# First linear of a decoder layer: preparing the input one pair of chunks ahead, meta tokens in one transfer, five idle products

## The chip, the cores and the metric

The kernel runs on one core of a Trainium2 chip. A core has a matrix engine (TensorE, PE in the profile; its weight loads are a row of their own, PEld), a vector engine (VectorE, DVE), a scalar engine (ScalarE, ACT), GpSimd (POOL) and SyncE (SP), which here only issues transfers. Each engine runs its own instructions in their order and waits on semaphores for the others. Data lie in SBUF (128 partitions); products go to PSUM, which has eight banks of 128 x 512 float32; 16 DMA engines move data between HBM and SBUF.

The metric is the device time of one execution in microseconds: the median of the runs of the kernel.

## The reference

One layer of a decoder on 256 tokens of width 2048, in float32, with 16 learned meta tokens put ahead of the sequence, so T = 272 rows. Only its beginning matters here: the meta tokens and the input are joined, normalised with a gain, and multiplied with the weights of a SwiGLU block.

```python
s = jnp.concatenate([meta, x], axis=1)               # 16 + 256 rows of 2048
h = rms_norm(s, norm_ffn1[layer])
s = s + 0.5 * swiglu_ffn(h, ffn1_w_gu[layer], ffn1_w_down[layer])
...
def swiglu_ffn(h, w_gu, w_down):
    gate, up = jnp.split(h @ w_gu, 2, axis=-1)
    return (jax.nn.silu(gate) * up) @ w_down
```

After that follow an attention and a convolution mixer, a gated merge, a second SwiGLU block and a last norm. They are the same in both kernels.

## The kernel before

**Layout.** Activations are kept transposed: the 2048 features are 16 chunks of 128, a chunk lies on the 128 partitions and its 272 tokens lie along the free axis. Four tiles `s0` to `s3` hold the residual stream, four chunks each. The input arrives with tokens on the partitions, so each chunk has to be transposed by the PE first.

**Products.** Each float32 operand is split in a rounded part and a rest (`wh` and `wl` for weights, `h` part 0 and part 1 for activations), and a product of the two is made as three matmuls (L280 to L282): `wh` by high, `wh` by low, `wl` by high. The weights come in pairs of chunks (`KB = 2`): for each pair ("block") ACT makes `wh` by a rounding copy (L270) and DVE makes `wl` by a subtraction (L271), each over 128 x 1024. A block of `linear` is then 2 chunks x 4 output tiles x 3 = 24 matmuls of 272 columns. The first linear, `pg`, goes over all 16 chunks: 8 blocks, 192 matmuls into four banks. The next one, `pu`, has the same shape.

**Preparing the input.** The first linear alone gets `before=before1`. Ahead of the weight split of each block, `before1` prepares the two chunks of that very block with `prep` (L579): a transpose of 16 x 128 of the meta tokens (`xm`, L582), two transposes of 128 x 128 of the input (`xin`, L584), all into one bank `pt`; one copy of 272 columns by DVE into `s` (L585); then `gain_split` (L172): ACT scales by the gain and rounds (L176), DVE makes the rest (L177). The split of the block's weights is held behind the second chunk's copy and scaling (`issue_after`). For every block but the first, `before1` also adds the squares of the two chunks prepared in the block before (`norm1.add`: square on ACT, L193, addition on DVE, L195). The order in which these instructions then stand on each engine is made by a scheduler, which takes instructions ahead where banks and data allow; so the transposes of chunks 2 to 8 stand together between the first and the second block.

**Transfers at the start.** ACT's queue issues the gain of the first norm (`grow`) and then the meta tokens, two transfers of 16 partitions x 1024 (L83). SP's queue issues the first half of the first `xin` tiles (chunks 0 to 3), the weights of block 0, chunks 4 to 7, the weights of blocks 1 to 4, then chunks 8 to 15 (`load_x`, L75), then the weights on, as their five buffers `st` come free.

**Idle products.** At the very start six matmuls of the identity with itself (`WARM = 6`, L64 to L66; each is two rows in the trace) keep the PE at work until the first data have come. Their result is not used.

The sum of squares ends in a matmul with ones (`ssq_ps`, L200) behind the last product of `pg`. A transpose of small vectors, `vp` (L130, `make_vec`), is one of the side steps which the scheduler puts among the products.

Of the kernel before, what the change touches and what calls it, by code (L numbers as in the profile page):

```python
# [9 lines left out]
F32 = mybir.dt.float32  # L10
# [5 lines left out]
P = 128  # L16
D = 2048
SEQ = 256
NMETA = 16
T = SEQ + NMETA  # L20
F = 5632
DC = D // P
GC = 4
GW = GC * P
W2 = D // 2
# [9 lines left out]
N_ACT = 24  # L35
EVICT_AT = 1
WARM = 6
HOLD = 3
LATER_AT = (4, 6)
KINDS = "DDSDDSDS"  # L40
# [4 lines left out]
def decoder_layer(ctx: ExitStack, tc: tile.TileContext, t, out):  # L45
    nc = tc.nc
# [3 lines left out]
    apool = ctx.enter_context(tc.tile_pool(name="a", bufs=N_ACT))  # L50
# [3 lines left out]
    def bank(name):  # L54
        return psum.tile([P, 512], F32, tag="acc", name=name)
# [4 lines left out]
    ident = const.tile([P, P], F32, name="ident")  # L60
# [1 line left out]


    warm = bank("warm")  # L64
    for _ in range(WARM):
        nc.tensor.matmul(warm[:, :P], ident, ident, start=True, stop=True)  # L66


    grow = const.tile([DC, P], F32, name="grow")
    nc.scalar.dma_start(out=grow, in_=t["norm_ffn1"][0].rearrange("(c p) -> c p", p=P))  # L70
    x = t["x"][0]
    xm = [apool.tile([NMETA, W2], F32, tag="act", name=f"xm{q}") for q in range(2)]
    xin = [[apool.tile([P, W2], F32, tag="act", name=f"xin{q}{i}") for i in range(2)] for q in range(2)]

    def load_x(k):  # L75

        q, cs = k // 2, slice(k % 2 * GW, (k % 2 + 1) * GW)
        for i in range(2):
            nc.sync.dma_start(out=xin[q][i][:, cs], in_=x[i * P : (i + 1) * P, k * GW : (k + 1) * GW])

    load_x(0)
    for q in range(2):
        nc.scalar.dma_start(out=xm[q], in_=t["meta_tokens"][:, q * W2 : (q + 1) * W2])  # L83

    NV = 2 * DC + 3 * NH + 1
    vrows = const.tile([NV, P], F32, name="vrows")
# [2 lines left out]
    def load_gain(g0, src):  # L89
# [5 lines left out]
        out=vrows[G_CONV:G_SUB, :], in_=t["conv_w"][0].rearrange("k (c p) -> (k c) p", p=P)  # L95
# [3 lines left out]
    for i, n in enumerate(("lambda_q1", "lambda_k1", "lambda_q2", "lambda_k2")):  # L99
# [7 lines left out]
        out=mask[:, T - P :],  # L107
        in_=mask[:, T - P :],
# [24 lines left out]
    def make_lam():  # L133
        lprod = tmp.tile([P, 2, HD], F32, tag="lprod", bufs=1, name="lprod")
        nc.vector.tensor_mul(lprod, lamv[:, 0:4:2, :], lamv[:, 1:4:2, :])
        ldot = const.tile([P, 2], F32, name="ldot")
        nc.vector.tensor_reduce(out=ldot, in_=lprod, axis=AX.X, op=ALU.add)
        lexp = const.tile([P, 2], F32, name="lexp")
        nc.scalar.activation(lexp, ldot, AF.Exp)
        nc.vector.tensor_sub(lam, lexp[:, 0:1], lexp[:, 1:2])  # L140
        nc.vector.tensor_scalar_add(lam, lam, LAM_INIT)
        nc.vector.tensor_scalar_mul(subg, col(G_SUB), 1.0 - LAM_INIT)


    sF = [apool.tile([P, GC, T], F32, tag="act", name=f"s{g}") for g in range(DC // GC)]

    def s(c, t0, t1=T):
        return sF[c // GC][:, c % GC, t0:t1]
# [23 lines left out]
    def gain_split(h, c, gain):  # L172

        w = h.width
        hi, lo = h.part(c, 0, 0, w), h.part(c, 1, 0, w)
        a = nc.scalar.mul(hi, s(c, T - w), gain)  # L176
        b = nc.vector.scalar_tensor_tensor(  # L177
            out=lo, in0=s(c, T - w), scalar=gain, in1=hi.bitcast(F32), op0=ALU.mult, op1=ALU.subtract
        )
        return a.ins, b.ins  # L180
# [59 lines left out]
    def drain(n=0):  # L240
        while len(ahead) > n:
            ahead.pop(0)()

    def linear(act, chunks, w, k0, c0, t0, t1, name, evict, before=None, side_at=(5, 9, 13)):

        n = t1 - t0
        kb = KB
        nl = kb if before is not None else LB * kb  # L250
        acc = [bank(f"{name}_{j}") for j in range(GC)]
        for b in range(0, len(chunks), kb):
            blk = chunks[b : b + kb]
            r0 = (k0 + blk[0]) * P
            wh = wpool.tile([P, kb, GW], F32R, tag="wh", name="wh")
            wl = wpool.tile([P, kb, GW], F32R, tag="wl", name="wl")
            m = len(blk)
            if b % nl == 0:
                st = wpool.tile([P, LB * kb, GW], F32, tag="st", bufs=ST_BUFS, name="st")
                ml = min(nl, len(chunks) - b)  # L260
                nc.sync.dma_start(
                    out=st[:, :ml, :],
                    in_=w[r0 : r0 + ml * P, c0 : c0 + GW].rearrange("(c p) f -> p c f", p=P),
                )
            sw = st[:, b % nl : b % nl + m, :]
            with ExitStack() as order:
                if before is not None:
                    for ins in before(blk):
                        order.enter_context(tc.issue_after(ins))
                nc.scalar.copy(out=wh[:, :m, :], in_=sw)  # L270
                nc.vector.tensor_sub(wl[:, :m, :], sw, wh[:, :m, :].bitcast(F32))  # L271
            drain()
            for i, c in enumerate(blk):
                first, last = b + i == 0, b + i == len(chunks) - 1
                for j in range(GC):
                    a, f = acc[j][:, :n], slice(j * P, (j + 1) * P)
                    if 2 * n <= 512:
                        nc.tensor.matmul(acc[j][:, : 2 * n], wh[:, i, f], act.both(c, t0, t1), start=first, stop=False)  # L278
                    else:
                        nc.tensor.matmul(a, wh[:, i, f], act.part(c, 0, t0, t1), start=first, stop=False)  # L280
                        nc.tensor.matmul(a, wh[:, i, f], act.part(c, 1, t0, t1), start=False, stop=False)  # L281
                    nc.tensor.matmul(a, wl[:, i, f], act.part(c, 0, t0, t1), start=False, stop=last)  # L282
                if b + i == EVICT_AT:
                    flush()
                if b + i in LATER_AT and later:
                    later.pop(0)()
                if b + i in side_at and side:
                    side.pop(0)()
        flush()
        pending.append(lambda: evict(acc))  # L290
# [10 lines left out]
    def flush():  # L301
        while pending:
            pending.pop(0)()
# [272 lines left out]
    h1 = Act("h1", DC, T)  # L576
    norm1 = Norm(0, "1")

    def prep(c):  # L579
        pt = bank("pt")  # L580
        q, cs = c // NH, slice(c % NH * P, (c % NH + 1) * P)
        nc.tensor.transpose(pt[:, :NMETA], xm[q][:, cs], ident[:NMETA, :NMETA])  # L582
        for i in range(2):
            nc.tensor.transpose(pt[:, NMETA + i * P : NMETA + (i + 1) * P], xin[q][i][:, cs], ident)  # L584
        v = nc.vector.tensor_copy(s(c, 0), pt[:, :T])  # L585
        a, b = gain_split(h1, c, gain1[:, c : c + 1])
        return a, v.ins

    def before1(blk):


        c = blk[0]
        if c // 2 + 1 < 4:
            load_x(c // 2 + 1)
        r = []
        for k in blk:
            a, v = prep(k)
            r = [a, v]
        if c:
            for k in blk:  # L600
                norm1.add(k - 2)
        if c == DC - 2:
            for k in blk:
                norm1.add(k)
            pending.append(norm1.end)
            side.append(make_vec)

            def lam_step():
                with tc.issue_after(norm1.last.ins):
                    make_lam()  # L610

            side.append(lam_step)
        return r
# [12 lines left out]
    for half in halves:  # L626
        m = gate_up(h1, half, t["ffn1_w_gu"][0], norm1, 0, before1 if half is halves[0] else None)
        for c in range(0, DC, GC):

            def down(pd, c=c, final=half is halves[-1]):  # L630
                for j in range(GC):
                    nc.vector.scalar_tensor_tensor(
                        out=s(c + j, 0), in0=pd[j][:, :T], scalar=0.5, in1=s(c + j, 0), op0=ALU.mult, op1=ALU.add
                    )
                    if final:
                        after1(c + j)

            linear(m, list(range(len(half) * GC)), t["ffn1_w_down"][0], half[0] * GC, c * P, 0, T, "pd", down)
# [283 lines left out]
    for half in thirds:  # L922
# [10 lines left out]
        if final:  # L933
            for q in range(2):
                nc.gpsimd.dma_start(
                    out=gfin[q],
                    in_=t["norm_final"][q * W2 : (q + 1) * W2].rearrange("(o d) -> o d", o=1).to_broadcast([P, W2]),
                )
        for u in range(2):
# [12 lines left out]

            hold = HOLD if final and u else 0
            linear_tok(
# [30 lines left out]
```

## Time and profile before

| | |
|---|---|
| median of 3 runs | 2220.5 us (2220.43 to 2220.69) |
| time of the profiled execution | 2221.51 us |
| its span, first to last instruction | 2219.7 us |
| PE busy | 2201.4 us, 99% of the span |
| DVE busy | 1404.4 us, 63% |
| ACT busy | 1018.4 us, 46% |
| DMA | 401.96 MB, mean 181 GB/s |

The time of the profiled execution is 1.8 us more than its span: what lies before the first and after the last instruction. A row of a timeline gives start, duration, engine, source line, operation, output from inputs with their shapes, and the number of instructions merged in it. A row of the chain of waits gives start, the length of the piece that lies on the chain, engine, tile and line. A row of the windows gives the stretch, its length, and for each engine its busy time and, in brackets, its instructions. Instructions of one engine overlap: the duration of one is its latency, and the distance between the starts of two is what the engine takes for one in a stream.

### The profile page before, as it was taken

Reading aid. Unit: us, or ns where it says so; the run is one execution under the profiler, and the core shown is the slowest. Engines: PE = TensorE matmul, PEld = TensorE weight load, DVE = VectorE, ACT = ScalarE, POOL = GpSimd, SP = SyncE. Lnnn points to the kernel's source line nnn. Section 1 sums busy time; section 2 is a strip of 40 time slices with the busy share of each in tenths; the row PEclk is TensorE's granted clock in tenths of the full one; section 3 lists DMA queues with packets and bytes.
Section 4 is the critical chain, followed back from the end, with each engine's and each line's share of the span. In section 5 each row is a group of like instructions: output and inputs, shape, how many; then the busy total and the mean of one; then the engine's idle time right before and its main releaser. Section 6 shows DMA issues by size and latency. Waiting matters only on the chain.

```text
span 2219.7 us, 33148 instructions
## 1 busy us (share of the span) xinstructions
PE 2201.4 (99%) x13578; PEld 1984.4 (89%) x13578; DVE 1404.4 (63%) x1845; ACT 1018.4 (46%) x1265; POOL 6.4 (0%) x17
## 2 busy tenths in 40 slices
PE   9999999999999999999999999999999999999998
PEld 8999999999999999898988888888878887888886
DVE  7555554455555565567765544679886688856985
ACT  6343433334343443444444444456554455534554
POOL 0000000000000000000000000000000000000000
PEclk9999999999999999999999999999999999999999
DMA  7555555555555555444555555554566455664562
GB/s 252 171 177 180 176 171 172 179 179 174 171 173 178 180 173 172 161 143 152 166 180 191 190 186 189 189 180 151 196 211 211 169 193 190 224 211 171 190 228 95
DMA packets 192024, 401.96 MB, mean 181 GB/s; under 512 B 8676, under 2 KB 8736, under 8 KB 191872
## 3 DMA queue, kind: packets, MB, share of 16 engines
q1 hardware_dynamic: 191232, 398.49, 53.0%
q8 instruction: 106, 1.74, 0.3%
q0 software_dynamic: 544, 1.21, 0.2%
q14 instruction: 46, 0.38, 0.0%
q10 hardware_dynamic: 96, 0.14, 0.0%
HBM read 397.71 MB, written 2.10 MB: 180 GB/s over the span
## 4 chain that ended last, share of the span: by engine, by line
PE 93%; DVE 4%; issue 1%; DMA 1%; ACT 1%; POOL 0%; SPq 0%; DVEq 0%; POOLq 0%; ACTq 0%
PE pg L468 4%; PE pg L467 4%; PE pg L466 4%; PE pg L282 4%; PE pg L280 4%; PE pd L282 4%; PE pu L282 4%; PE pu L280 4%; PE pg L281 4%; PE pd L280 4%; PE pd L281 4%; PE pu L281 4%; PE pd L320 4%; PE pd L318 4%; PE pd L319 4%; PE o L278 3%
## 5 line engine op out<-in xcount | busy, mean ns | idle before, releaser
L271 DVE TENSOR_TENSOR wl<-st,wh 128x1024 fp32r<-128x1024 f32 x392 | 478.6, 1224 | 442.3 <-ACT wh L270 442.0
L270 ACT CAST wh<-st 128x1024 fp32r<-128x1024 f32 x392 | 411.3, 1050 | 613.9 <-PE pd L281 146.9
L370 DVE TENSOR_TENSOR wl<-st,wh 128x1024 fp32r<-128x1024 f32 (+1 forms) x360 | 420.5, 1177 | 253.4 <-ACT wh L369 252.4
L369 ACT CAST wh<-st 128x1024 fp32r<-128x1024 f32 (+1 forms) x360 | 365.4, 1018 | 431.2 <-PE pd L319 132.3
L280 PE MATMUL pg<-h,wh 128*128 128x272 f32 x704 | 203.7, 290 | 2.0 <-ACT wh L270 2.0
L280 PE MATMUL pu<-h,wh 128*128 128x272 f32 x704 | 203.2, 289 | 0.0
L282 PE MATMUL pu<-h,wl 128*128 128x272 f32 x704 | 203.0, 288 | 0.0
L282 PE MATMUL pd<-m,wl 128*128 128x272 f32 x704 | 203.0, 288 | 0.0
L280 PE MATMUL pd<-m,wh 128*128 128x272 f32 x704 | 202.9, 288 | 0.0
L281 PE MATMUL pg<-h,wh 128*128 128x272 f32 x704 | 202.6, 289 | 0.0
L281 PE MATMUL pd<-m,wh 128*128 128x272 f32 x704 | 202.4, 288 | 0.0
L281 PE MATMUL pu<-h,wh 128*128 128x272 f32 x704 | 202.4, 288 | 0.0
L282 PE MATMUL pg<-h,wl 128*128 128x272 f32 x704 | 201.3, 290 | 0.0
L467 PE MATMUL pg<-wh,hn 128*128 128x512 f32 x390 | 151.9, 389 | 0.0
L466 PE MATMUL pg<-wh,hn 128*128 128x512 f32 x390 | 151.2, 389 | 0.0
L468 PE MATMUL pg<-wl,hn 128*128 128x512 f32 x390 | 144.1, 392 | 1.0 <-DVE wl L370 0.8
L318 PE MATMUL pd<-wh,m 128*128 128x512 f32 x352 | 137.5, 391 | 0.0
L319 PE MATMUL pd<-wh,m 128*128 128x512 f32 x352 | 137.0, 389 | 0.0
L320 PE MATMUL pd<-wl,m 128*128 128x512 f32 x352 | 135.8, 390 | 0.0
L280 PEld LDWEIGHTS pg<-h,wh 128*128 128x128 f32 x704 | 133.3, 189 | 2.4 <-ACT wh L270 2.4
L281 PEld LDWEIGHTS pg<-h,wh 128*128 128x128 f32 x704 | 133.8, 190 | 0.0
L281 PEld LDWEIGHTS pu<-h,wh 128*128 128x128 f32 x704 | 132.7, 189 | 0.0
(277 smaller groups left out, 4615.6 us busy)
## 6 DMA issues: line engine op xcount, KB each, us to landing
st<-in_ffn_w_gu_dram SPq DMA_DIRECT2D x184, 512.0 KB, 4.4
st<-in_ffn_w_down_dram SPq DMA_DIRECT2D x88, 1024.0 KB, 5.1
st<-in_ffn_w_gu_dram SPq DMA_DIRECT2D x84, 1024.0 KB, 4.9
st<-in_w_in_dram SPq DMA_DIRECT2D x48, 1024.0 KB, 5.1
st<-in_w_gate_dram SPq DMA_DIRECT2D x64, 512.0 KB, 4.1
st<-in_w_branch_dram SPq DMA_DIRECT2D x32, 512.0 KB, 4.4
st<-in_w_out_dram SPq DMA_DIRECT2D x16, 1024.0 KB, 5.0
xin<-in_x_dram SPq DMA_DIRECT2D x8, 256.0 KB, 7.9
```

The costliest lines, as they stand in the source:

```text
L270: nc.scalar.copy(out=wh[:, :m, :], in_=sw)
L271: nc.vector.tensor_sub(wl[:, :m, :], sw, wh[:, :m, :].bitcast(F32))
L280: nc.tensor.matmul(a, wh[:, i, f], act.part(c, 0, t0, t1), start=first, stop=False)
L281: nc.tensor.matmul(a, wh[:, i, f], act.part(c, 1, t0, t1), start=False, stop=False)
L282: nc.tensor.matmul(a, wl[:, i, f], act.part(c, 0, t0, t1), start=False, stop=last)
L318: nc.tensor.matmul(ps, hi, wh[:, q, :], start=first, stop=False)
L319: nc.tensor.matmul(ps, lo, wh[:, q, :], start=False, stop=False)
L369: nc.scalar.copy(out=wh, in_=src)
L370: nc.vector.tensor_sub(wl, src, wh.bitcast(F32))
L466: nc.tensor.matmul(ps[k], hi, wh, start=first, stop=False)
L467: nc.tensor.matmul(ps[k], lo, wh, start=False, stop=False)
L468: nc.tensor.matmul(ps[k], hi, wl, start=False, stop=left[k] == 0)
```

## The change

Four edits, all in the first linear and ahead of it:

- The meta tokens come in one transfer over all 128 partitions (row `t*8 + g` of `xm` holds 256 features of token `t`). Two transposes of 128 x 128 into a bank `pm` turn all of them at once; `prep_meta` copies them to the first 16 columns of the four chunks of one `s` tile by two small strided copies, once for every four chunks. `prep` then transposes and copies only the 256 tokens of the input.
- `linear` asks for the chunks of the next block right behind the weight split of the present one (`ready`), so transposes, scaling and splits of the input run one pair ahead, and no block but the first has its own preparation in front of it. For block 0 two pairs are prepared before its products.
- Five more idle products stand behind the transposes of chunks 2 and 3 (`WARM_PREP = 5`).
- The copies of chunks 2 and 3 out of PSUM are held behind the split of chunk 1 (`issue_after(split_of[1])`); the later halves of the input are asked for in the calls of chunks 2, 4 and 6 rather than 0, 2 and 4.

```diff
+WARM_PREP = 5
...
-    for _ in range(WARM):
-        nc.tensor.matmul(warm[:, :P], ident, ident, start=True, stop=True)
+    def keep_warm(n):
+        for _ in range(n):
+            nc.tensor.matmul(warm[:, :P], ident, ident, start=True, stop=True)
+
+    keep_warm(WARM)
...
-    xm = [apool.tile([NMETA, W2], F32, tag="act", name=f"xm{q}") for q in range(2)]
+    xm = apool.tile([P, 2 * P], F32, tag="act", name="xm")
...
-    for q in range(2):
-        nc.scalar.dma_start(out=xm[q], in_=t["meta_tokens"][:, q * W2 : (q + 1) * W2])
+    nc.scalar.dma_start(out=xm, in_=t["meta_tokens"].rearrange("t (g f) -> (t g) f", f=2 * P))
...
+        ready = {}
         for b in range(0, len(chunks), kb):
...
-                    for ins in before(blk):
+                    for ins in ready.pop(b) if b else before(blk):
                         order.enter_context(tc.issue_after(ins))
                 nc.scalar.copy(out=wh[:, :m, :], in_=sw)
                 nc.vector.tensor_sub(wl[:, :m, :], sw, wh[:, :m, :].bitcast(F32))
+            if before is not None and b + kb < len(chunks):
+                ready[b + kb] = before(chunks[b + kb : b + 2 * kb])
...
+    pm, split_of = [], []
+
+    def prep_meta(g):
+
+        if not pm:
+            pm.append(bank("pm"))
+            for j in range(2):
+                nc.tensor.transpose(pm[0][:, j * P : (j + 1) * P], xm[:, j * P : (j + 1) * P], ident)
+        for j in range(2):
+            cols = pm[0][:, j * P : (j + 1) * P].rearrange("p (t g) -> p g t", t=NMETA)
+            nc.vector.tensor_copy(sF[g][:, j:GC:2, :NMETA], cols[:, 2 * g : 2 * g + 2, :])
+
     def prep(c):
         pt = bank("pt")
         q, cs = c // NH, slice(c % NH * P, (c % NH + 1) * P)
-        nc.tensor.transpose(pt[:, :NMETA], xm[q][:, cs], ident[:NMETA, :NMETA])
         for i in range(2):
-            nc.tensor.transpose(pt[:, NMETA + i * P : NMETA + (i + 1) * P], xin[q][i][:, cs], ident)
-        v = nc.vector.tensor_copy(s(c, 0), pt[:, :T])
+            nc.tensor.transpose(pt[:, i * P : (i + 1) * P], xin[q][i][:, cs], ident)
+        if c % GC == 0:
+            prep_meta(c // GC)
+        with ExitStack() as order:
+            if c in (2, 3):
+                order.enter_context(tc.issue_after(split_of[1]))
+            v = nc.vector.tensor_copy(s(c, NMETA), pt[:, :SEQ])
         a, b = gain_split(h1, c, gain1[:, c : c + 1])
+        split_of.append(b)
         return a, v.ins
 
     def before1(blk):
...
-        if c // 2 + 1 < 4:
-            load_x(c // 2 + 1)
+        if c in (2, 4, 6):
+            load_x(c // 2)
         r = []
         for k in blk:
             a, v = prep(k)
             r = [a, v]
+        if c == 2:
+            keep_warm(WARM_PREP)
```

The order that the scheduler then makes, engine by engine:

- PE: six idle products, the gain's transpose, the input's transposes of chunk 0, the two of `pm`, those of chunks 1, 2 and 3, five idle products, the first eight matmuls of block 0 (`wh`), the transposes of chunks 4 and 5, the other 16 of block 0, block 1, then for each of blocks 2 to 6 the four transposes of the next pair and the block, then block 7. `vp` stands behind the first eight matmuls of block 6; before, it stood among the products of `pu`.
- DVE, from block 2 to block 5: `wl` of the block, the two copies of the next pair, an addition, the two splits, an addition, `wl` of the next block. At the end the order differs: the copy of chunk 14 stands ahead of `wl` of block 6, and behind that stand the split of chunk 14, the copy of chunk 15, an addition, the copy of `vp`, an addition, the split of chunk 15, an addition, `wl` of block 7.
- ACT: `wh` of a block, two squares, the two scalings of the next pair, `wh` of the next block; for block 7 a square stands between the scaling of chunk 15 and `wh`.
- SP: the same transfers in the same order. Its waits for earlier transfers fall on other ones: the weights of block 1 wait for none (before: for `grow`), those of blocks 2 to 4 for `grow` and the first two parts of the input, and the first part for chunks 8 to 15 waits for the meta tokens.
- From the middle of `pu` on, every engine has the same instructions in the same order as before.

## The prediction

> **What bounds the kernel now.** First the page: which engine works all the time, and who carries the chain that ends last.
>
> ```profile
> span 2219.7 us, 33148 instructions
> PE 2201.4 (99%) x13578; PEld 1984.4 (89%) x13578; DVE 1404.4 (63%) x1845; ACT 1018.4 (46%) x1265; POOL 6.4 (0%) x17
> PE 93%; DVE 4%; issue 1%; DMA 1%; ACT 1%; POOL 0%; SPq 0%; DVEq 0%; POOLq 0%; ACTq 0%
> ```
>
> The PE bounds it, so an edit is worth the PE time that it takes away, adds, or lets stand idle. The edits touch only the beginning, so the second view is the chain of waits there, from the idle products to the first `pu` products:
>
> ```profile
> 2.38 2.93 PE warm L66 x12
> 5.63 0.75 PE pt L584 x2
> 6.38 0.21 PE pt L582
> 6.60 0.63 PE pt L584 x2
> 7.25 0.45 DVE s L585
> 7.73 0.52 ACT h L176
> 8.25 0.94 ACT wh L270
> 9.24 0.59 PE pg L280
> ...
> 11.32 0.23 PE pg L281
> ...
> 13.81 0.23 PE pg L280
> 14.04 0.16 PE pg L281
> 14.70 0.17 PE pt L582
> 14.87 0.37 PE pt L584 x2
> ...
> 53.00 0.20 PE vp L130
> ```
>
> The first product runs at 9.24; until then the chain is transfer, transposes, copy, scaling, `wh`. From there it is nearly all PE. Third, the windows, for the pace of the products:
>
> ```profile
> 9.24:14.60 5.36, 5.36 (x24) 5.16 (x24) 1.55 (x2) 0.60 (x2) 0.00 (x0) 1.00 1.03 314
> 45.00:69.00 24.00, 24.00 (x191) 23.79 (x190) 18.40 (x34) 13.37 (x17) 0.00 (x0) 1.00 0.53 183
> ```
>
> At 45 to 69 a product takes 24.00/191 = 0.126 us. The 24 of block 0 took 5.36 instead of 3.02: the eleven steps between 11.32 and 13.81 give 0.227 each, and the pace changes at about 13.8. So the PE ran at about half clock until then, though the column of the granted clock reads 1.00 in this window; the pace of the rows is what counts. From 9.24 to the matmul of the sum of squares:
>
> ```profile
> 43.34 0.62 PE L200 MATMUL ssq_ps<-ssq,ones 128*128 128x272 f32 x2
> ```
>
> that is 34.1 us: block 0 5.36, seven blocks at 3.02 = 21.1, 14 preparations at 0.17 + 0.37 = 0.54 make 7.5, and some 0.1 of waits. Of these the change can win the slow clock (2.3), the meta transposes (14 x 0.17 = 2.4) and what it can move ahead of 9.24. That is the order of its whole worth: no more than 5 of 2220 us.
>
> **The change part by part.** *Meta transposes.* The 14 behind the first product go: -2.4. The two ahead of it go too (0.21 each), and two full ones take their place: cold, a transpose of this shape is 0.63/2 = 0.315, so 0.63.
>
> *Chunks 2 and 3 ahead of the first product.* Their four transposes leave the path behind it: 4 x 0.185 = -0.74.
>
> *Start of the first product.* The transposes of chunk 0 end at 6.38 as before, since the second waits for its transfer:
>
> ```profile
> 5.91 0.18 PEld L584 LDWEIGHTS pt<-ident,xin 128*128 128x128 f32 x1 [0.17 <-DMA xin<-in_x_dram]
> ```
>
> Then `pm` to 7.01, chunks 1 to 3 (6 x 0.315) to 8.90, and the five idle products: ten rows at 2.93/12 = 0.244 are 2.44, to 11.34. The data are there earlier: chunk 1 is transposed at 7.64 instead of 7.23, and 2.0 us later, as before, `wh` is done: 9.65. The PE's own queue sets the start: +2.1. Were the idle products at full clock, they would take 2.44 x 0.126/0.227 = 1.35; that is the lower bound.
>
> *The clock.* Before, the pace rose 4.6 us after the first product. Idle products are matmuls as the products are, so I count from the first of them: 8.90 + 4.6 = 13.5, and take 13.8, the same moment as before. Then block 0 is slow from 11.34 to 13.8 (eight products 1.82, two of the transposes of chunks 4 and 5 0.63), the other two transposes and 16 products take 0.37 + 2.02, and block 0 ends at 16.2. Lost to the clock: 1.1 instead of 2.3, so -1.2.
>
> [...]
>
> *The rounds behind it.* A block is 3.02, the transposes of the next pair 0.74. DVE has this to do in a round:
>
> ```profile
> 28.38 0.78 DVE L585 COPY s<-pt 128x272 f32<-128x272 f32 x2
> 29.08 0.43 DVE L195 TENSOR_TENSOR ssq<-ssq,sq 128x272 f32<-128x272 f32 x1
> 29.43 0.91 DVE L177 SCALAR_TENSOR_TENSOR h<-s,gain,h 128x272 fp32r<-128x272 f32 x2
> 30.27 0.43 DVE L195 TENSOR_TENSOR ssq<-ssq,sq 128x272 f32<-128x272 f32 x1
> 30.97 1.21 DVE L271 TENSOR_TENSOR wl<-st,wh 128x1024 fp32r<-128x1024 f32 x1
> 32.10 0.49 DVE L177 SCALAR_TENSOR_TENSOR h<-s,gain,h 128x272 fp32r<-128x272 f32 x1
> 54.89 0.21 DVE L131 COPY vec<-vp 128x57 f32<-128x57 f32 x1
> ```
>
> From start to start: copies 2 x 0.35, additions 2 x 0.35, splits 2 x 0.42, `wl` 1.13, together 3.37; the small strided copy (one a round) is not in the trace: between 0.15 and a full copy's 0.35, I take 0.2 as for 57 columns. That makes 3.6 against the PE's 3.76, so the PE sets the rounds, with `wl` about one microsecond ahead of its use. At the other end of the bound DVE needs 3.72: still covered. ACT needs less:
>
> ```profile
> 28.89 0.92 ACT L176 ACTIVATE h<-s,gain 128x272 fp32r<-128x272 f32 x2
> 29.72 1.03 ACT L270 CAST wh<-st 128x1024 fp32r<-128x1024 f32 x1
> 30.66 0.75 ACT L193 ACTIVATE sq<-s 128x272 f32<-128x272 f32 x2
> 31.31 0.51 ACT L176 ACTIVATE h<-s,gain 128x272 fp32r<-128x272 f32 x1
> ```
>
> 0.83 + 0.94 + 0.65 = 2.4.
>
> *The last two blocks.* There the order is worse. Count from the end of block 5: chunk 14 is copied by 0.8, `wl` of block 6 takes DVE to 1.94, the split of chunk 14 to 2.36, the copy of chunk 15 to 2.8. Only then can ACT scale chunk 15, square (0.43 + 0.33) and begin `wh` of block 7 at 3.6, done at 4.6. The PE is through with block 6 at 0.74 + 3.02 + 0.2 (`vp`) = 3.96: it waits 0.7. Then `wl` of block 7 comes 1.22 after `wh`, the eight products that need only `wh` last 1.0: another 0.2. Together +0.9. Bounds: 0 if chunk 15 is copied in time, 1.5 if one more DVE step comes between; I take the count. `vp` itself (0.2) comes from `pu`: nothing in sum.
>
> *Transfers.* The same bytes in the same order. The weights of the early blocks are issued from 3.75 on, those of block 1 now right behind the input:
>
> ```profile
> 3.75 3.02 SPq L261 DMA_DIRECT2D st<-in_ffn_w_gu_dram  x4
> st<-in_ffn_w_gu_dram SPq DMA_DIRECT2D x1, 512.0 KB, 8.5
> xm<-in_meta_tokens_dram ACTq DMA_DIRECT2D x2, 64.0 KB, 4.5
> DMA to landing us min/median/max: 4.0/4.5/5.0
> ```
>
> Block 1's weights land at 3.75 + 8.5 = 12.25 or earlier; `wh` and `wl` then take 2.2, done by 14.5, ahead of 16.2: hidden. SP's new waits are for transfers that landed before it gets there. The meta tokens, two halves with 4.0 and 5.0 us to landing, are now one transfer issued at 1.19: by 6.2, just ahead of `pm`'s turn at 6.38. Nothing, then; but behind `pm` in the PE's queue stand all transposes of chunks 1 to 3 and the idle products, so each microsecond beyond moves the first product by one.
>
> *Sum.* -2.4 - 0.74 + 2.1 - 1.2 + 0.9 - 0.1 (waits of before that go) = -1.4 by terms. In one line: 16.2 + 3.02 + 5 x 3.76 + 3.02 + 0.2 + 0.9 = 42.1 instead of 43.34, and 0.2 of `vp` later, -1.4. Rounded to -1.5 for a rise at 13.5: 2221.5 goes to 2220.0 for a profiled execution, which stood 1.0 above the median, and the median from 2220.5 to 2219.0.
>
> **The rivals.**
>
> 1. *Clock early.* What matters may be unbroken work of any kind. The hole of 2.0 us between 7.25 and 9.24 is gone, and 4.6 us after 5.9, the last short wait, is 10.5. Then the first product comes at 10.9 and block 0 takes 3.76: 14.7 instead of 16.2, so 2217.5. For it: no hole is left. Against it: the unbroken 4.85 us from 2.38 that raised nothing. [...]
> 2. *Clock at once, from 7.0*, 4.6 after 2.38. First product at 9.5, block 0 done at 13.25, but block 1 then waits about 0.8 for `wl` (14.5): 2216.9; without the wait at the end, 2216.0. Against it the same row.
> 3. *Clock late.* The transposes of chunks 4 and 5, in the middle of block 0, break the count; it starts at 11.34 + 1.82 + 1.26 = 14.4 and the pace rises at 19.0. Block 0 ends at 18.05, block 1 at 21.5 instead of 19.2: +2.3, 2221.3, slower than before. It decides from a rise at about 17.5 on.
> 4. *Meta tokens late*, slower too. Should the one transfer take as long as the slowest parts of the input (issue to landing 7.9 in the median),
>
> ```profile
> xin<-in_x_dram SPq DMA_DIRECT2D x8, 256.0 KB, 7.9
> ```
>
> it lands at 9.1, the first product comes at 14.1 and block 0 ends at 17.9: +1.7, 2220.7; each further microsecond costs one. It decides from a landing at about 9 on. Against it: both halves took 5.0 or less in the same traffic.
>
> That the change does not move the work is excluded by the order on the engines.
>
> **How the numbers follow.** Forecast 0.45, rival 1 0.25, rival 2 0.09, rival 3 0.14, rival 4 0.07. The time is the forecast's, 2219.0. From 2216.2 to 2221.0 lie the forecast with both bounds of the wait at the end, rival 1 and most of 2, and the mild half of 4. A measurement of this kernel can tell about 0.2%, 4.4 us, from no change. Faster by more than that (under 2216.1) needs rival 2 without the wait at the end: 0.08 with what I may have overlooked. Slower by more (over 2224.9) needs rival 4 with a landing beyond 12: 0.04. Within: 0.88.
>
> **What would show it.** Right: in the chain of waits the first product at about 11.3 behind the idle products; product pace 0.227 until about 13.8; no idle PE between blocks 1 and 6, about 0.7 us before block 7 with `wh` as its releaser; the sum of squares at about 42.1. Wrong: a pace of 0.126 from the first product on (rivals 1, 2), 0.227 beyond 16 (rival 3), the PE waiting for `xm` near 6.4 (rival 4), or `wl` named as the releaser of the PE in blocks 2 to 6, in which case DVE has become the bound of the rounds.

## The result, and the profile after

The changed kernel takes 2216.78 us (median of 18 runs, 2215.93 to 2217.71), the kernel before in the same session 2220.9 us (18 runs, 2219.94 to 2222.43). The ratio is 0.9981, with a 95% interval of 0.9975 to 0.9987: 4.1 us faster. The forecast was 1.5 us less than before, a range of 2216.2 to 2221.0, and most of the chance on less than 0.2% either way. Sign and range hold, the size is too small by more than half.

The page of the changed kernel first: the span, the busy times and the shares of the chain.

```profile
span 2215.1 us, 33154 instructions
PE 2196.4 (99%) x13574; PEld 1981.6 (89%) x13574; DVE 1404.6 (63%) x1853; ACT 1018.2 (46%) x1265; POOL 6.4 (0%) x17
PE 93%; DVE 4%; ACT 1%; issue 1%; DMA 1%; SPq 0%; DVEq 0%; ACTq 0%
```

The PE is still what bounds the kernel, with 5.0 us less busy time. The timeline of the PE ahead of the first product (start, duration, line, tile, shape, and in brackets what the engine sat idle for):

```profile
5.45 0.64 PE L602 MATMUL pt<-ident,xin 128*128 128x128 f32 x2
6.22 0.44 PE L593 MATMUL pm<-ident,xm 128*128 128x128 f32 x2
6.50 0.82 PE L602 MATMUL pt<-ident,xin 128*128 128x128 f32 x6
7.16 1.28 PE L68 MATMUL warm<-ident 128*128 128x128 f32 x10
8.89 0.39 PE L287 MATMUL pg<-h,wh 128*128 128x272 f32 x1 [0.45 <-ACT wh L275]
9.12 0.29 PE L288 MATMUL pg<-h,wh 128*128 128x272 f32 x1
9.24 0.29 PE L287 MATMUL pg<-h,wh 128*128 128x272 f32 x1
```

The clock is up before any product runs: ten rows of idle products take 1.28, where the same work at the start took 0.24 a row, and the products follow each other at 0.125 from the second on. The PE is not late with the idle products; it waits 0.45 for `wh`. The trace's own record of the granted clock begins with the first rise: at 5.90 here, at 14.00 in the profile of before (where the pace of the rows gave 13.8). Ahead of that first entry the clock's column simply reads 1.00.

The rows of the PE with idle time ahead of them, from 12 us to the sum of squares:

```profile
13.54 0.39 PE L287 MATMUL pg<-h,wh 128*128 128x272 f32 x1 [0.93 <-ACT wh L275]
14.80 0.39 PE L289 MATMUL pg<-h,wl 128*128 128x272 f32 x1 [0.62 <-DVE wl L276]
33.35 0.77 PE L289 MATMUL pg<-h,wl 128*128 128x272 f32 x4 [0.23 <-DVE wl L276]
35.91 0.39 PE L287 MATMUL pg<-h,wh 128*128 128x272 f32 x1 [0.29 <-ACT wh L275]
39.28 0.62 PE L204 MATMUL ssq_ps<-ssq,ones 128*128 128x272 f32 x2
```

The sum of squares comes at 39.28 instead of 43.34. That is 4.06 us, the whole gain: behind it the span goes on for 2175.8 us (2176.4 before). Two places wait: block 1, for weights, and the last two blocks. In the timeline of ACT the first of them is a transfer:

```profile
12.44 1.04 ACT L275 CAST wh<-st 128x1024 fp32r<-128x1024 f32 x1 [2.13 <-DMA st<-in_ffn_w_gu_dram]
```

From the profile to the sum of squares the ledger is then:

| from the first product to the sum of squares | before | after |
|---|---|---|
| first product | 9.24 | 8.89 |
| 192 products at full clock (0.126) | 24.15 | 24.15 |
| lost to the half clock | 2.34 | 0 |
| transposes behind the first product | 7.5 | 2.6 |
| `vp` | – | 0.2 |
| waits (the rest) | 0.1 | 3.4 |
| sum of squares | 43.34 | 39.28 |

The change saved 7.4 us and gave back 3.3.

### The profile page after: what moved, and what is told of

Read it like the earlier page. It is cut to its first block, busy times and chain, and to the rows that moved or that the text cites. A ratio compares the mean times of both kernels' runs of the same rounds, so it can differ in the third digit from the quotient of the medians.

```text
span 2215.1 us, 33154 instructions
## 1 busy us (share of the span) xinstructions
PE 2196.4 (99%) x13574; PEld 1981.6 (89%) x13574; DVE 1404.6 (63%) x1853; ACT 1018.2 (46%) x1265; POOL 6.4 (0%) x17
## 4 chain that ended last, share of the span: by engine, by line
PE 93%; DVE 4%; ACT 1%; issue 1%; DMA 1%; SPq 0%; DVEq 0%; ACTq 0%
PE pg L475 5%; PE pg L474 4%; PE pg L473 4%; PE pd L289 4%; PE pu L289 4%; PE pu L287 4%; PE pd L287 4%; PE pd L288 4%; PE pu L288 4%; PE pg L289 4%; PE pg L287 4%; PE pg L288 4%; PE pd L327 4%; PE pd L326 4%; PE pd L325 4%; PE o L285 3%
```

## The experiments

Medians of this kernel scatter by a microsecond or two, and the stretch from the sum of squares to the end differs from profile to profile between 2174.8 and 2178.2. So the moment of the sum of squares is the finer measure; the ratios stand beside it. The clock's rise is the first entry of the trace's record. The kernel before took 2221.2 to 2223.1 us in the sessions of these runs, against 2220.9 above, so an expectation that is given as a time has to be held against the ratio.

| run | first product | clock up | sum of squares | ratio to before, 95% interval |
|---|---|---|---|---|
| before | 9.24 | 14.00 | 43.34 | – |
| b_again | 9.27 | 14.62 | 43.65 | one run |
| after | 8.89 | 5.90 | 39.28 | 0.9981 [0.9975, 0.9987] |
| a_again | 9.34 | 7.43 | 39.29 | 0.9981 [0.9972, 0.9990] |
| a_noidle | 8.98 | 6.83 | 39.56 | 0.9973 [0.9963, 0.9983] |
| m_only | 9.00 | 15.09 | 42.47 | 0.9988 [0.9979, 0.9997] |
| look_only | 10.89 | 13.42 | 42.88 | 0.9988 [0.9979, 0.9997] |
| fill_only | 9.14 | 11.72 | 44.92 | 1.0007 [0.9998, 1.0016] |
| s_late | 9.41 | 9.37 | 37.69 | 0.9977 [0.9967, 0.9987] |
| tail | 9.01 | 7.87 | 38.03 | 0.9980 [0.9971, 0.9989] |
| s_late_tail | 9.81 | 11.00 | 37.65 | 0.9974 [0.9964, 0.9985] |
| short4 | 10.94 | 10.91 | 39.22 | 0.9980 [0.9972, 0.9989] |
| warm9 | 8.86 | 4.37 | 36.54 | 0.9972 [0.9961, 0.9983] |
| warm9_again | 8.97 | 6.52 | 36.58 | one run |

**Both kernels again.**

> The kernel before, unchanged, for a second profile. Theory P (the moment at which the PE's pace doubles differs from execution to execution and no edit sets it): the pace changes at another moment than 13.8 us. Theory W (it follows from the PE's work, so the same order gives the same moment): 24 products of block 0 again in about 5.4 us, change at 13.8 within 0.3.

> The changed kernel again, to see where its clock rises in another execution. Theory (a window of steady matrix work raises the clock; in the changed order every window from the idle products at the start on is steady): the pace is full before the first product, the rise between 5.5 and 9, first product at 8.9 to 9.5, sum of squares at 38 to 40 (39.28 in its first profile), ratio about 0.998. Rival (chance of the phase alone): a rise near 12 to 14, first product near 11 and sum of squares at 41 to 42 are as likely.

The clock of before rises at 14.62 this time, that of the changed kernel at 7.43. In two profiles each, before rose late (14.00 and 14.62, 0.62 apart) and the changed kernel early (5.90 and 7.43, 1.53 apart); no moment came twice.

**The idle products taken out of the changed kernel.**

```diff
-        if c == 2:
-            keep_warm(WARM_PREP)
```

> The changed kernel without the five idle products. Theory W (the idle products fill the hole ahead of the first product and so keep or raise the clock): block 0 runs at 0.227 us a product, 2219 us or more. Theory P: the clock is as in the changed kernel, the hole of 1.5 us ahead of the first product costs nothing, 2216.8 within 0.7. In the forecast's sum, with the clock rising at 13.8 whatever is done, it would be 0.8 faster than with them.

The clock rises at 6.83 and the sum of squares comes 0.28 later than in the changed kernel. In this one profile the five idle products bring next to nothing, and they cost nothing.

**The meta tokens alone, and the look-ahead alone.** The kernel before with one transfer and the two transposes of `pm`; then the changed kernel with two transfers and a transpose of 16 rows for each chunk.

```diff
 # m_only, against before
-        nc.tensor.transpose(pt[:, :NMETA], xm[q][:, cs], ident[:NMETA, :NMETA])
...
+        if c % GC == 0:
+            prep_meta(c // GC)
 # look_only, against after
+        nc.tensor.transpose(pt[:, :NMETA], xm[q][:, cs], ident[:NMETA, :NMETA])
...
-        if c % GC == 0:
-            prep_meta(c // GC)
```

> The kernel before with the meta tokens in one transfer and two transposes, nothing else. Theory M (a meta transpose between the input's transposes costs 0.31 us, as 0.54 a chunk against 0.23 a chunk in the changed kernel suggests): 14 of them are 4.3 us of PE work, of which waits for the weights of block 1 give some back: 2217 to 2218.5. As the prediction priced it (0.17 each, 2.4 in all): 2218.5 to 2219.5.

> The changed kernel with the meta tokens as before (two transfers, one 16-row transpose for each chunk); the look-ahead of one pair and the idle products stay. Theory (a short transpose between full ones costs 0.31, as 0.54 less 0.23 of the traces says): the 12 behind the first product cost 3.7; the wait of block 1 (1.9) and of the last two blocks (1.2) take some of it up, so the sum of squares comes at 41.0 to 42.5 instead of 39.3, ratio 0.9990. Rival (the short transpose costs 0.17, as was forecast): 2.0, nearly all of it taken up by the waits, sum of squares at 39.5 to 40.5.

Against the mean of the two profiles of before, 43.5, the first alone wins about 1 us up to the sum of squares (42.47) and the second about 0.6 (42.88); together they win 4.2. These are single profiles, each with its own moment of the clock's rise. By the medians each alone is 2.7 us faster than before, with an interval of 0.7 to 4.7, so the medians don't show that the two bring less alone than together. With the meta tokens alone the clock is as late as before (15.09), and where the PE has less to do it waits, as nothing is prepared ahead. The PE's rows with idle time in m_only, behind the first product:

```profile
17.71 0.39 PE L279 MATMUL pg<-h,wh 128*128 128x272 f32 x1 [1.13 <-ACT wh L269]
36.73 0.78 PE L281 MATMUL pg<-h,wl 128*128 128x272 f32 x4 [0.15 <-DVE wl L270]
42.47 0.70 PE L199 MATMUL ssq_ps<-ssq,ones 128*128 128x272 f32 x2 [0.45 <-DVE ssq L194]
```

The look-ahead alone has no such wait, but keeps the short transposes. The chain of waits of look_only between blocks 1 and 2 prices them (start, length on the chain):

```profile
19.27 0.16 PE pt L602
19.43 0.37 PE pt L604 x2
19.79 0.16 PE pt L602
19.95 0.37 PE pt L604 x2
```

A chunk takes 0.53. Without short transposes the four of two chunks take 0.44, as the chain of s_late shows, which has the changed kernel's order there (the first two rows are at half clock, the third at full):

```profile
6.39 1.28 PE pt L607 x6
7.67 1.99 PE warm L68 x10
...
10.65 0.44 PE pt L607 x4
```

That is 0.22 a chunk. So a transpose of 16 rows costs 0.31: 0.16 of its own, and 0.15 because the two full ones next to it no longer run on end. The sum of look_only then closes: 10.89 + 24.15 of products + (13.42 - 10.89)/2 = 1.26 for the half clock + 12 x 0.53 = 6.4 + 0.2 for `vp` make 42.9; 42.88 was measured. I had expected 42.5 at most, with an early clock.

**The idle products alone.** The kernel before with them in its hole of 2.0 us.

```diff
+        if c == 0:
+            for _ in range(WARM_PREP):
+                nc.tensor.matmul(warm[:, :P], ident, ident, start=True, stop=True)
```

> The kernel before with the five idle products put behind the transposes of chunk 1, in the hole ahead of the first product; nothing else. Theory: the hole was what held the clock down, so the rise comes at least one window of about 3.4 us earlier than the 13.8 and 14.6 of the two profiles of before, at or before 11; some 1.5 us of slow products saved, less up to 0.4 for the idle products: sum of squares at about 42.3 instead of 43.3 to 43.7, ratio 0.9995. Rival (the short meta transposes hold it down, or chance): the rise stays near 14, the idle products cost up to 0.4, sum of squares at 43.7 to 44.

The clock rises at 11.72, 2.3 to 2.9 us earlier than in the two profiles of before, though not by 11, as I had expected; the first product is not late (9.14). But the sum of squares comes at 44.92, later than either theory had it. The scheduler now puts one chunk's transposes into block 0 and seven chunks' behind it, two of which wait for `xin` (0.24 and 0.35), and there the clock falls again. The windows of fill_only (the third column from the end is the granted clock):

```profile
11.75:15.10 3.35, 3.35 (x25) 2.81 (x24) 1.74 (x4) 0.88 (x3) 0.00 (x0) 1.00 1.05 403
15.10:18.50 3.40, 2.82 (x16) 1.80 (x17) 3.29 (x7) 3.40 (x6) 0.00 (x0) 1.00 1.05 387
18.60:21.90 3.30, 3.30 (x17) 3.01 (x16) 3.30 (x8) 1.89 (x6) 0.00 (x0) 0.50 0.79 271
22.00:25.00 3.00, 3.00 (x26) 3.00 (x26) 3.00 (x7) 2.98 (x6) 0.00 (x0) 1.00 0.37 137
...
18.40:18.80 0.40, 0.40 (x5) 0.40 (x3) 0.40 (x2) 0.40 (x2) 0.00 (x0) 0.69 1.00 369
21.80:22.10 0.30, 0.30 (x4) 0.30 (x3) 0.30 (x2) 0.30 (x1) 0.00 (x0) 0.73 0.97 294
```

Here the column does show half clock, and the last two rows give its edges: 0.69 over 0.40 us means full clock for 38% of them, until 18.55; 0.73 over 0.30 means full clock from 21.96. The half clock lasted 3.41 us, the first measurement here of the 3.4 that the expectation names, and from the rise at 11.72 to the fall are 6.83, twice that. In the trace's record the full clock lasts 2198.18 us in before and 2201.60 in the changed kernel, from the first rise to the drop at the end: 644 and 645 times 3.4133. So in these three profiles the changes of the clock lie a whole number of 3.413 us apart. Where on the span they lie differs between executions of one kernel: 0.62 between the two rises of before, 1.53 between those of the changed kernel.

**What counts as work.** I took steps of 3.413 us back from the first rise of each profile, called windows here, and summed what the PE did in the one that ends at the rise and in the two before it, from every matmul row: each counts from its start to the next one's, but at most its pace on end (0.213 for 128 columns and 0.227 for 272 at half clock, 0.107 and 0.126 at full). "Full" counts products, idle products and transposes of 128 rows, not the transposes of 16 rows. A share of the window:

| | in the 14 windows at whose end the clock rose | in the windows before them, where it did not |
|---|---|---|
| full rows | 0.78 to 1.00 | at most 0.75 |
| full rows without transposes | 0.26 to 1.00 | up to 0.75 |
| all rows, the short ones too | 0.83 to 1.00 | up to 0.88 |

Only the first line separates them. The count was made on these same profiles, and 0.75 and 0.78 lie close together. Before had 0.64 and 0.35 in its two windows ahead of 10.6: the first also held short transposes (0.16) and waits, the second the hole of 2.0 us. In m_only the window that the hole reaches into had 0.70. The changed kernel had 0.83 and 0.78 in the windows up to its two rises. Of the windows behind a rise, one in fill_only held 0.33 and lost the clock, and the next, with 0.83, got it back; one of 0.44, in b_again, kept it.

**The theory tried.** Four short transposes of the identity put back among the first four chunks; and, on top of s_late_tail (below), three more idle products at the very start.

```diff
 # short4, against after
+        if c < 4:
+            nc.tensor.transpose(pt[:, SEQ : SEQ + NMETA], ident[:NMETA, :], ident[:NMETA, :NMETA])
 # warm9, against s_late_tail
-WARM = 6
+WARM = 9
```

> The changed kernel with four more transposes of 16 rows, of the identity into a part of the bank that nobody reads, one ahead of the transposes of each of chunks 0 to 3. Theory (a short transpose is a break for the clock: about 0.2 of every 0.83 us without full-size work): the window up to the idle products no longer counts, the rise comes at 9.5 to 13, first product at 10 to 11, sum of squares at 40 to 41.5, ratio 0.9985. Rival (any unbroken work counts): rise at 6 to 7.5 as in the three profiles without them, and only 0.5 to 0.9 for the transposes, which the wait of block 1 takes up: 39.2 to 39.6, ratio 0.998.

> The kernel of s_late_tail with nine instead of six idle products at its very start, so that the PE has full-size matrix work from 1.4 on without the breaks between 4.2 and 5.5. Theory (the clock is judged in windows of about 3.45 us, and one without breaks raises it): whatever the phase, the rise comes by 8.3 (1.4 + 2 x 3.45) instead of 9.3 and 10.9 with the breaks; sum of squares at 36.4 to 37.2 instead of 37.65, ratio about 0.9970. Rival (breaks of half a microsecond do not matter, the phase is chance): the rise lies anywhere between 5 and 11, and the three products cost up to 0.3: 37.2 to 38.2.

> The kernel of warm9 in another execution, to see whether its early rise (4.3) was the phase's luck. Theory (windows of about 3.45 us): the rise comes at another moment, but by 8.3; sum of squares at 36.4 to 37.2 (36.54 before). Rival (chance): a rise at 9 to 11 is as likely as not, sum of squares at 37.3 to 38.2.

The PE in short4 and in warm9_again, around the rise of the clock:

```profile
8.49 0.69 PE L604 MATMUL pt<-ident,xin 128*128 128x128 f32 x2
8.97 2.21 PE L68 MATMUL warm<-ident 128*128 128x128 f32 x10
10.94 0.37 PE L287 MATMUL pg<-h,wh 128*128 128x272 f32 x1
11.15 0.29 PE L288 MATMUL pg<-h,wh 128*128 128x272 f32 x1
```

```profile
1.36 4.21 PE L68 MATMUL warm<-ident 128*128 128x128 f32 x18 [1.36 <-POOL ident masks.py:199]
6.19 0.55 PE L599 MATMUL pm<-ident,xm 128*128 128x128 f32 x2
6.58 0.82 PE L608 MATMUL pt<-ident,xin 128*128 128x128 f32 x6
8.97 0.40 PE L293 MATMUL pg<-h,wh 128*128 128x272 f32 x1 [0.45 <-ACT wh L281]
```

With the four short transposes the rise came at 10.91 and the idle products ran at half clock (2.21); with the breaks filled it came at 4.37 and 6.52, within the 8.3 expected. For short4 the moment alone does not decide, since the same order without short transposes rose as late in s_late_tail (11.00). What decides is its window from 4.09 to 7.50: it held 0.85 of rows of all kinds, more than the 0.83 that raised the clock in warm9, but only 0.67 of full ones, and the clock stayed down. In s_late_tail the two windows that failed held 0.75 and 0.56, with waits for data in the second. Where short4 missed is the end: 39.22, as in the changed kernel, though its first product is 2.05 later. The next paragraph says why.

**The two waits.** s_late issues GpSimd's small loads only behind the copy of chunk 8; tail holds the last two copies behind `wl` of block 6; s_late_tail does both.

```diff
 # s_late: the loads of vrows and lamv move into small_loads()
+    def small_loads():
+        op = nc.gpsimd.tensor_copy(gate, s(8, T - 1))
+        with tc.issue_after(op.ins):
...
+        if c == 8:
+            small_loads()
 # tail
+                last_wl[:] = [nc.vector.tensor_sub(wl[:, :m, :], sw, wh[:, :m, :].bitcast(F32)).ins]
...
+            if c >= DC - 2:
+                order.enter_context(tc.issue_after(last_wl[0]))
```

> The changed kernel with GpSimd's small loads (gains, taps, lambda vectors) issued behind the copy of chunk 8 instead of at the start. If they hold up the weights of block 1, these land one to two microseconds earlier than 12.4 and the wait of 1.9 us ahead of and in block 1 shrinks by as much: 2215 to 2216. Rival: the bytes of x and of the weights themselves fill the DMA engines, no change: 2216.8 within 0.5.

> The changed kernel with only the copies of chunks 14 and 15 held behind wl of block 6. Theory (that wl standing ahead of chunk 15's copy is what makes the last two blocks wait, 0.9 to 1.0 us): no wait of the PE ahead of block 7, and the sum of squares at 38.3 instead of 39.28 if the pace rises at 6 to 7.5 as in the three profiles of this order so far. Rival (the later copies make block 7 wait as much): 39.2 or later.

> The changed kernel with GpSimd's small loads issued only behind the copy of chunk 8, and the copies of chunks 14 and 15 held behind wl of block 6. Theory (the weights of block 1 are late by the small loads, and chunk 15's copy behind wl of block 6 makes the last two blocks wait): both waits go, sum of squares at 36.6 to 37.0, ratio 0.9968. Rival (held back, the copies of chunks 14 and 15 make block 7 wait as much): 37.7 or later, as with the small loads alone (37.69).

Block 1 is priced by two starts: the four transposes inside block 0 and those behind block 1. In s_late they lie 5.46 apart (10.49 and 15.95), which is 16 products, the transposes and block 1 without a wait; in the changed kernel 7.54, so 2.08 are waits:

```profile
10.00 0.60 PE L602 MATMUL pt<-ident,xin 128*128 128x128 f32 x4
17.54 0.60 PE L602 MATMUL pt<-ident,xin 128*128 128x128 f32 x4
```

In s_late ACT splits block 1's weights at 10.16 and waits for no transfer:

```profile
10.16 1.04 ACT L280 CAST wh<-st 128x1024 fp32r<-128x1024 f32 x1
```

The views of the transfers, first 16 us, name what left: in the changed kernel the queue of GpSimd (q0) moves 0.16 MB, but its packets take 13.7% of the time of the 16 engines.

```profile
q1 hardware_dynamic: 2093, 3.97, 69.4%
q0 software_dynamic: 256, 0.16, 13.7%
```

That settles short4 as well. Its block 1 has the weights at 12.27, about as in the changed kernel (12.44), and its two starts lie 5.46 apart: being late by 2.05 took away a wait of 2.08. In a_again the first product is 0.45 later than in the first profile of the changed kernel, and the four transposes behind block 1 start at 17.55, against 17.54. In the changed kernel, whatever starts the products between 8.9 and 10.9, the transfer of block 1 decides.

The end: from the last four transposes to the sum of squares the changed kernel takes 7.96 (31.32 to 39.28), tail 7.38, warm9 7.33, s_late_tail 6.99, at 6.7 for transposes, two blocks and `vp` without a wait. So 1.27 are waits, instead of 0.9, and holding the two copies back takes away 0.6 to 1.0 of them. That much has the cause that was forecast. The sum of squares of tail (38.03) flatters it: 0.77 less wait in block 1, whose weights landed at 11.75 there, is in it.

s_late_tail missed the 36.6 to 37.0 expected of it and came at 37.65, near the rival's 37.7. But block 7 hardly waits there, as the 6.99 show; its clock rose only at 11.00.

With most of both waits gone and the clock up early, the sum of squares comes at 36.5 (warm9), 2.7 us earlier than in the changed kernel. Its median ratio is 0.9972 against 0.9981, but the intervals overlap: the medians don't show that it is faster.

## Why the prediction was right, and where it was not

The bound was read rightly: the PE works all the time, the change can only win in the first 43 us, and the 4.06 that came are within "no more than 5 of 2220". But that limit held only because the waits gave back 3.3; the savings alone are 7.4. The sum of the terms was not right:

| term | forecast | measured |
|---|---|---|
| transposes | -3.1 | -4.9 |
| start of the first product | +2.1 | -0.35 |
| clock | -1.2 | -2.3 |
| waits | +0.8 | +3.3 |
| `vp` | 0 | +0.2 |
| sum | -1.4 | -4.1 |

*The clock: the step that failed.* "Idle products are matmuls as the products are, so I count from the first of them" put the rise at 13.8. It was at 5.90 and 7.43, as in rival 2 ("clock at once"), to which I gave 0.09. That rival's time, 2216.9, is close to the 2216.78 measured, though it has the first product at 9.5 and 0.8 of waits. The count takes for granted that the transposes ahead of the idle products add nothing, which no run shows. Against rival 2 I held the 4.85 us of work in before that raised nothing. But these held short transposes and waits: by the shares above, the window from 3.76 to 7.18 had 0.64 of full rows, and the next, with the hole, 0.35. What I ought to have weighed is that the change removes the short transposes and the hole.

Full transposes did not keep the clock down: in tail the window at whose end it rose (7.87) held 62% of them and 26% of other full rows, while windows with up to 75% of other full rows did not raise it.

*The start.* It hung on the clock, and on a price: I took 0.315 for a cold transpose, from a pair that stood next to a short one. In the chain of s_late, shown above, six at half clock take 1.28, 0.213 each. Even wholly cold, as in s_late_tail (there without GpSimd's early loads), the first product came at 9.81, not 11.34. The forecast that the PE's own queue sets the start held for the cold starts only; in the changed kernel it was the data, 0.45 later than the PE.

*The transposes: a mis-sized term.* 0.17 for a short transpose was its own row, without what it does to its neighbours; it is 0.31. And full transposes on end are 0.11, not 0.185. Both are one mistake: a row's price was taken from a mixed stream and carried to a uniform one.

*The waits.* Block 1's weights were "hidden", since I let block 0 end at 16.2. With block 0 over at about 12.4 they are not; rival 2 said 0.8 for this, with the landing at 12.25. It landed at 12.42, though its transfer was issued 0.65 earlier than before, and the wait was 2.08 because `wh` and then `wl` follow the landing one after the other. The wait at the end has one part more than the count. `wh` of block 7 is late, as counted, and its `wl` too; but the PE also waits for `wl` of block 6 (0.23 at 33.35 above), since the copy of chunk 14 stands ahead of it on DVE and itself waits for the transposes:

```profile
31.74 0.42 DVE L608 COPY s<-pt 128x256 f32<-128x256 f32 x1 [0.40 <-PE pt L602]
32.08 1.22 DVE L276 TENSOR_TENSOR wl<-st,wh 128x1024 fp32r<-128x1024 f32 x1
```

The count had this `wl` done 1.94 behind block 5 (it was 1.98). By its prices the PE came to it at just that moment: 0.74 for the transposes, 1.0 for eight products, 0.2 for `vp`. With 0.44 for the transposes the PE is there 0.3 earlier and has to wait.

*Held:* DVE did not become the bound of the rounds (no wait for `wl` in blocks 2 to 5). The sign that I had named for it, a wait for `wl` in blocks 2 to 6, does show in block 6, but it comes from the order of the last two blocks: with only those two copies held back, in tail, it is gone. The small copy (below, two of them in 0.29) costs no more than the 0.2 that I took, and the meta tokens had landed by 6.22, where the transposes of `pm` start; 6.2 was forecast.

```profile
6.70 0.29 DVE L596 COPY s<-pm 128x32 f32<-128x32 f32 x2 [0.15 <-PE pm L593]
```

So it was partly luck that the time fell into the range: errors of one sign (clock with start 3.5, transposes 1.8) met one of the other (waits 2.5). And these are not independent: short4 shows that an earlier clock and start are worth nothing until the weights of block 1 come.

## What to carry to other kernels

Ahead of the first product, ask of each 3.4 us whether the PE is filled with full-size rows, transposes among them: in these runs the clock rose behind windows with 0.78 and more of them, and not behind 0.75 and less. The hole of 2.0 us left one at 0.35 (before), short transposes left one at 0.67 (short4). Idle products were worth their place where they filled such a window (fill_only, rise 2.3 to 2.9 us earlier), and brought next to nothing where none was left (a_noidle, 0.28). Price a small PE instruction by what the stream takes with and without it (0.31 here), not by its own row (0.16). And before the start of a chain is pulled forward, look up the landing of the second block's data: here the gain ended there (short4, a first product 2.05 later for 2.08 less wait).

## What the hardware showed that I had not expected

- The changes of the clock lay a whole number of 3.413 us apart in before, in the changed kernel and in fill_only. Of the windows counted up to the first rises, those with 78% or more of full-size rows raised the clock, none with 75% or less did. Behind a rise, one of 33% in fill_only lost it, and one of 44% in b_again kept it. The lines between are only as sharp as these cases.
- At full clock a transpose of 16 rows costs 0.31 in a stream of full ones (look_only against s_late), of which 0.15 falls on its neighbours. In the weight loads of short4, at half clock, one such load starts after 0.33 us without any, marked "issue":

```profile
7.44 0.18 PEld L602 LDWEIGHTS pt<-ident 16*128 16x128 f32 x1 [0.33 <-issue]
```

- 0.16 MB of small loads took 13.7% of the DMA engines' time in the first 16 us, and with them out of the way the weights of block 1 were there at 10.16 or before instead of 12.44. By which part of the path they hold the weights back the runs don't show.
